# High and low parts of queries and keys: made once on all 128 partitions, put in place by transfers within SBUF

## The chip, the cores and the metric

The kernel runs on one core of one Trainium2 chip. The metric is the device time of one execution in microseconds. Three timed runs of the kernel before took 2474.62, 2475.18 and 2477.01 us; the median, 2475.18 us, is what the change is measured against.

## The reference

One layer of a streaming encoder, in float32: 2048 tokens, width 1024, 16 heads of 64. With `DEPTH = 1` only the chunked attention runs, followed by a SwiGLU network, each between two RMS norms.

```python
def chunk_relpos_attention(h, w_qkv, w_o, rel_bias):     # chunks of 64; each sees itself and the 8 before
    q, k, v = split_heads(h, w_qkv)
    for c in range(n_chunks):
        k0, k1 = max(0, (c - LEFT_CHUNKS) * CHUNK), (c + 1) * CHUNK
        sc = einsum('bhqd,bhkd->bhqk', q[c], k[:, :, k0:k1]) / 8 + bias
        outs.append(einsum('bhqk,bhkd->bhqd', softmax(sc), v[:, :, k0:k1]))
    return merge_heads(outs) @ w_o

def reference(x, ...):
    x = x + rms_norm(chunk_relpos_attention(rms_norm(x, g0), ...), g1)
    return x + rms_norm((silu(h @ w_gate) * (h @ w_up)) @ w_down, g3)     # h = rms_norm(x, g2)
```

## The kernel before

Every float32 product is made from rounded parts. A number is split into a high part (ACT copies it into the type float32r) and a low part (what is left, a subtraction on DVE), and a product is the three matmuls of L188 to L190: high by high, high by low, low by high.

The tokens are taken in two groups (g) of 1024, each of two halves (s) of 512. A group goes through the dense layers and the attention, eight pairs (p) of heads one after the other. For each pair and half `qk_job` makes the queries, then the keys: 24 matmuls of 128x512 into one PSUM bank (tile `mm`, two buffers in the attention stages), with head 0 of the pair on partitions 0 to 63 and head 1 on 64 to 127. ACT copies the bank to a tile `t` in SBUF (L467), and `keep_qk` makes from `t` the operands of the scores:

- `q`, 128 x 4 x 512: on partitions 0 to 63 the high part of the head's queries, on 64 to 127 the high part again; beside it the low part, on both halves too. Per head: two ACT copies (L479, L482), one DVE subtraction (L480) and one POOL copy (L481), all on 64 partitions.
- `k`, 128 x 2 x 1536: per head the high part on partitions 0 to 63 (L493, ACT) and the low part on 64 to 127 (L494, DVE). The first 512 columns are the last half of the group before, loaded from `kh`.

So one matmul over 128 partitions sums high queries by high keys and high queries by low keys (L531), and a second one does the same with the low queries (L532). `Attend.scores` does that for a block of 128 queries; the scores of a block go into one tile `st` (one buffer). DVE adds the bias and takes the row's maximum (L540), ACT makes exponentials (L544), POOL scales them by the reciprocal sum (L548). `transposed` turns the probabilities on TensorE into `tt` (L564, L575; two buffers), DVE and ACT copy them to `pT` (L567, L569, L576), and `output` multiplies by the values (L593).

TensorE's order is written out by hand: a loop over slots, four per job (a job is one half of one pair), puts the scores of the next block, pieces of dense work (`fill`), transposes and outputs one behind the other. The dense work for a job, `qk` above all, has a due slot, shortly before the job's first scores; `until(("qk", ...))` makes sure that it stands ahead of them. On the other engines a scheduler orders the instructions when the program is built, SP's transfers too; each engine works its own list in order. On SP, and so on one hardware queue, stand all loads and stores: weights (`raw`, each half waits for its buffer until the half before has been split, L124 and L125), bias tiles, `kh`, attention results (`attn`, `al`), sums. The shared buffers `io` (three) hold `t` and many loads; `q` and `k` have two buffers each.

After attention comes the network (from about 1110 us on), which the change does not touch.

Of the kernel before, what the change touches and what calls it, by code (L numbers as in the profile page):

```python
# [9 lines left out]
F32 = mybir.dt.float32  # L10
F32R = mybir.dt.float32r
AF = mybir.ActivationFunctionType
ALU = mybir.AluOpType
# [3 lines left out]
P = 128  # L17
# [6 lines left out]
HALF = 512  # L24
# [23 lines left out]
def trunk(  # L48
# [12 lines left out]
    pe, act, dve, pool = nc.tensor, nc.scalar, nc.vector, nc.gpsimd  # L61
# [12 lines left out]
    xp = ctx.enter_context(tc.tile_pool(name="xp", bufs=2))  # L74
# [103 lines left out]
    def dense_bank(n, wide=False):  # L178

        if "psf" in phase and n % 2:  # L180
            return phase["psf"].tile([P, HALF], F32, tag="pd", name="mm", bufs=6)
        if wide and n % 2:
            return phase["psa"].tile([P, 4, P], F32, tag="tt", name="mm", bufs=2).rearrange("p a b -> p (a b)")
        return ps.tile([P, HALF], F32, tag="mm", name="mm")

    def products(pt, a_hi, a_lo, b_hi, b_lo, first, last, go_on=False):

        pe.matmul(pt, a_hi, b_hi, start=first, stop=False, skip_group_check=go_on)  # L188
        pe.matmul(pt, a_hi, b_lo, start=False, stop=False, skip_group_check=go_on)  # L189
        pe.matmul(pt, a_lo, b_hi, start=False, stop=last, skip_group_check=go_on)  # L190
# [24 lines left out]
    def scratch(name):  # L215

        n = turn[0] % 9
        if "fp" in phase:
            turn[0] += 1
        if "fp" in phase and n >= 4:  # L220
            return phase["fp"].tile([P, HALF], F32, tag="tmp", name=name, bufs=5)
        return xp.tile([P, 640], F32, tag="sc", name=name, bufs=4)
# [120 lines left out]
    def hb_tile(n, dtype=F32R, shape=(2, 4, HALF)):  # L343

        n_ht[0] += 1
        pool_ = hp if n < 4 else phase["fp"]
        return pool_.tile([P, *shape], dtype, tag=f"hb{n}", name=f"hb{n}_{n_ht[0]}", bufs=1)
# [63 lines left out]
    heads = (slice(0, 64), slice(64, 128))  # L411
# [7 lines left out]
    def bias_tile(n, h):  # L419

        if len(bias_bufs) < 4:
            t = phase["ap"].tile([P, 640], F32, name=f"bias{h}", bufs=1)
            pool.memset(t[0:64, 0:64], -BIG)
            pool.memset(t[64:128, 576:640], -BIG)
            bias_bufs.append(t)
        t = bias_bufs[n % 4]
        for n, c in enumerate((slice(64, 640), slice(0, 576))):
            e = ext_d[h : h + 1, 64 * n + c.start : 64 * n + c.start + 1]
            sp.dma_start(
                t[64 * n : 64 * n + 64, c],  # L430
                bass.AP(tensor=e.tensor, offset=e.offset, ap=[[1, 64], [1, c.stop - c.start]]),
            )
        return t
# [22 lines left out]
    def qk_job(g, s, p, w):  # L456
        ht = hts[s]
        for which in range(2):
            pt = dense_bank(which, (s, p) == (0, 0))
            c = slice(which * P, which * P + P)  # L460
            for k in range(KT):
                products(
                    pt, w.hi(k, c), w.lo(k, c), ht.hi(k), ht.lo(k), k == 0, k == KT - 1
                )
                yield 3 * C512
            t = xp.tile([P, HALF], F32, tag="io", name="t", bufs=3)
            act.activation(t, pt, AF.Copy, scale=(0.125, 1.0)[which])  # L467
            keep_qk(g, s, p, which, t)

    def keep_qk(g, s, p, which, t):  # L470

        ap = phase["ap"]
        a, b = heads
        if which == 0:

            q = ap.tile([P, 4, HALF], F32R, tag="q", name=f"q_{g}_{s}_{p}", bufs=2)
            qs[g, s, p] = q
            for h, own in enumerate(heads):
                act.activation(q[a, h, :], t[own, :], AF.Copy)  # L479
                dve.tensor_tensor(q[a, 2 + h, :], t[own, :], q[a, h, :].bitcast(F32), op=ALU.subtract)  # L480
                pool.tensor_scalar(q[b, h, :], t[own, :], 1.0, 1.0, op0=ALU.mult, op1=ALU.mult)  # L481
                act.activation(q[b, 2 + h, :], q[a, 2 + h, :].bitcast(F32), AF.Copy)  # L482
            return

        here = slice((s + 1) * HALF, (s + 2) * HALF)
        if s == 0:
            kk = ap.tile([P, 2, 3 * HALF], F32R, tag="k", name=f"k_{g}_{p}", bufs=2)
            ks[g, p] = kk
            if g > 0:
                sp.dma_start(kk[:, :, 0:HALF].bitcast(F32), khist_d[g - 1][p])  # L490
        kk = ks[g, p]
        for h, own in enumerate(heads):
            act.activation(kk[a, h, here], t[own, :], AF.Copy)  # L493
            dve.tensor_tensor(kk[b, h, here], t[own, :], kk[a, h, here].bitcast(F32), op=ALU.subtract)  # L494
        if s == 1 and g + 1 < NG:
            sp.dma_start(khist_d[g][p], kk[:, :, here].bitcast(F32))

    class Attend:
# [14 lines left out]
        def scores(self, ib):  # L513
            g, s, p = self.g, self.s, self.p
            ap = phase["ap"]
            if (g, p, "bias") not in bias:
                bias[g, p, "bias"] = [bias_tile(NH * g + 2 * p + h, 2 * p + h) for h in range(2)]
            q, kk = qs[g, s, p], ks[g, p]
            cols = slice(ib * P, ib * P + P)
            if self.prev:  # L520
                n, k0 = 640, s * HALF + ib * P
                cuts = [(P, 512, 768), (768, 1024, 1408)]
            else:
                n, k0 = (ib + 1) * P, HALF
                cuts = [(0, n), (512, 512 + n)]
            st = phase["psa"].tile([P, 3 * HALF], F32, tag="S", name="st", bufs=1)
            for h in range(2):
                c0 = cuts[h][0]
                for a, b in zip(cuts[h][:-1], cuts[h][1:]):
                    key = slice(k0 + a - c0, k0 + b - c0)  # L530
                    pe.matmul(st[:, a:b], q[:, h, cols], kk[:, h, key], start=True, stop=False)  # L531
                    pe.matmul(st[:, a:b], q[:, 2 + h, cols], kk[:, h, key], start=False, stop=True)  # L532
            for h in range(2):
                c0 = cuts[h][0]
                sc = scratch("sc")
                nmax = ap.tile([P, 1], F32, tag="nmax", name="nmax", bufs=4)
                rows = ap.tile([P, 2], F32, tag="rows", name="rows", bufs=4)
                t = bias[g, p, "bias"][h]
                rev = t[:, n - 1 :: -1] if n == 640 else t[:, 0:n][:, ::-1]
                dve.tensor_tensor_reduce(  # L540
                    out=sc[:, :n], in0=st[:, c0 : c0 + n], in1=rev, scale=-1.0, scalar=3.0e38,
                    op0=ALU.add, op1=ALU.min, accum_out=nmax,
                )
                act.activation(  # L544
                    sc[:, :n], sc[:, :n], AF.Exp, bias=nmax, scale=-1.0, accum_out=rows[:, 0:1]
                )
                dve.reciprocal(rows[:, 1:2], rows[:, 0:1])  # L547
                last_pool[0] = pool.tensor_scalar(  # L548
                    sc[:, :n], sc[:, :n], rows[:, 1:2], 1.0, op0=ALU.mult, op1=ALU.mult
                )  # L550
                self.sc[ib, h] = sc
# [576 lines left out]
    def begin(weights):  # L1128

        ap = phase["ap"]  # L1130
        a, b = heads
        u = Cols(0)
        stage = hb_tile(2, F32, (KT, HALF))
# [6 lines left out]
        for k in range(KT):  # L1140
            if k % 2 == 0:
                s = slice(k * 256, k * 256 + 512)
                sp.dma_start(raw[:, s], plan[0][:, s])
                to = ready[0][k // 4]
                part = slice(k % 4 * 256, k % 4 * 256 + 512)
                split_part(to[0][:, part], to[1][:, part], raw[:, s])
            h = stage[:, k, :]
# [8 lines left out]
        for c in range(2):  # L1156
            s = slice(c * 1024, c * 1024 + 1024)
            part = raw[:, 2048 + c * 1024 : 3072 + c * 1024]
# [9 lines left out]
        for which in range(2):  # L1168
            pt = ps.tile([P, HALF], F32, tag="mm", name="pqk")
# [16 lines left out]
        for t2 in range(2):  # L1186
            pt = phase["psa"].tile([P, 2, 256], F32, tag="tt", name="pv_", bufs=2)
# [9 lines left out]
        ts = []  # L1197
        for which in range(2):
            t = xp.tile([P, HALF], F32, tag="io", name="t", bufs=3)
# [1 line left out]
            ts.append(t)  # L1201
        drain()
        for which in range(2):
            keep_qk(0, 0, 0, which, ts[which])
        weights.extend((qw, vw))
        again = Prep(0, x[0], PRE_MIX)
        again.r = rstd
# [2 lines left out]
    def dense():  # L1210

        halves = [slice(0, HALF), slice(HALF, GROUP)]
        for g in range(NG):
            for p in range(NPAIR):
# [29 lines left out]
                for s in range(2):  # L1244
                    yield from qk_job(g, s, p, qw)
                    said.add(("qk", g, s, p))
# [245 lines left out]
```

## Time and profile before

| | |
|---|---|
| median of three runs | 2475.18 us |
| the profiled execution's own time | 2472.72 us |
| its span, first to last instruction | 2470.8 us |
| PE busy | 2412.7 us, 98% |
| DVE, ACT, POOL busy | 1515.2, 1149.3, 352.2 us |
| moved by DMA | 440.14 MB |
| mean granted TensorE clock | 0.993 |

The page lists, for groups of instructions, line, engine, operation, output and input, shape, count, then the busy time and the mean of one, then how long the engine stood idle just before them and what ended that. "PEld" is the load of weights into TensorE, which overlaps its matmuls; "SPq" is SP issuing a transfer. A busy time of PE counts pipelined matmuls, whose records overlap; where PE truly waited, a timeline row has the wait and its releaser in brackets at its end.

### The profile page before, as it was taken

How to read it: one execution, taken by the hardware profiler on the slowest of the kernel's cores; microseconds unless marked ns; L12 is line 12 of the kernel's file. 1: busy time of each engine (PE TensorE's matmuls, PEld its weight loads, DVE VectorE, ACT ScalarE, POOL GpSimd, SP SyncE). 2: the span in 40 equal slices, each digit the busy share in tenths (PEclk: the TensorE clock that was granted, in tenths of full speed). 3: DMA queues.
4: the chain of work that ended last, by engine and by line, in shares of the span. 5: the costliest groups of instructions: out<-in, count | busy, mean ns of one | idle time of the engine just before them, and what ended most of it. 6: DMA issues, size and time to landing. Idle time of an engine off the chain costs nothing.

```text
span 2470.8 us, 34560 instructions
## 1 busy us (share of the span) xinstructions
PE 2412.7 (98%) x12536; PEld 1996.1 (81%) x12536; DVE 1515.2 (61%) x2616; ACT 1149.3 (47%) x1991; POOL 352.2 (14%) x434
## 2 busy tenths in 40 slices
PE   7999999899999999999999999999999999999997
PEld 5888878688878887878888888888888888888886
DVE  6655455567565655568566655577656655555567
ACT  5545454554555545464433343356443333334444
POOL 3223233301333332220000000000000000000001
PEclk9999999999999999999999999999999999999999
DMA  5336666855666654347667755377667665457654
GB/s 176 120 111 164 147 167 165 247 182 166 156 165 168 155 137 118 82 121 242 187 206 223 251 172 187 99 251 246 206 221 249 203 204 158 132 175 235 195 188 149
DMA packets 184794, 440.14 MB, mean 178 GB/s; under 512 B 20752, under 2 KB 22816, under 8 KB 183344
## 3 DMA queue, kind: packets, MB, share of 16 engines
q1 hardware_dynamic: 174832, 403.33, 50.4%
q0 software_dynamic: 9792, 34.61, 8.6%
q8 instruction: 99, 1.62, 0.3%
q14 instruction: 71, 0.58, 0.1%
HBM read 358.64 MB, written 148.42 MB: 205 GB/s over the span
## 4 chain that ended last, share of the span: by engine, by line
PE 52%; DVE 1%; DMA 1%; issue 0%; ACT 0%; DVEq 0%; SPq 0%; ACTq 0%
PE pd L189 5%; PE pd L188 5%; PE pd L190 5%; PE pb L188 5%; PE pb L189 5%; PE pb L190 5%; PE pa L188 3%; PE pa L190 3%; PE pa L189 3%; PE pc L188 3%; PE pc L190 3%; PE pc L189 3%; PE mm L188 1%; PE mm L190 1%; PE mm L189 1%; DMA raw<-gu_S 0%
## 5 line engine op out<-in xcount | busy, mean ns | idle before, releaser
L188 PE MATMUL mm<-hb,whi 128*128 128x512 f32 x720 | 298.5, 415 | 2.4 <-ACT hb L340 2.4
L189 PE MATMUL mm<-hb,whi 128*128 128x512 f32 x720 | 284.2, 395 | 2.6 <-DVE hb L341 1.8
L190 PE MATMUL mm<-hb,wlo 128*128 128x512 f32 x720 | 284.2, 395 | 0.0
L548 POOL TENSOR_SCALAR sc<-sc,rows 128x640 f32<-128x640 f32 (+4 forms) x256 | 194.7, 765 | 602.4 <-DVE rows L547 548.6
L544 ACT ACTIVATE sc<-sc,nmax 128x640 f32<-128x640 f32 (+4 forms) x256 | 193.2, 755 | 187.1 <-DVE nmax L540 185.5
L540 DVE CUSTOM_DVE_ANT_0 sc<-st,bias 128x640 f32<-128x640 f32 (+4 forms) x256 | 180.3, 738 | 99.7 <-PE st L532 97.3
L188 PE MATMUL pb<-hb,whi_gu_T 128*128 128x512 f32 x528 | 206.3, 391 | 3.1 <-DVE terms L952 3.1
L190 PE MATMUL pb<-hb,wlo_gu_T 128*128 128x512 f32 x528 | 205.5, 389 | 0.0
L189 PE MATMUL pb<-hb,whi_gu_T 128*128 128x512 f32 x528 | 205.5, 389 | 0.0
L258 POOL TENSOR_TENSOR rs<-ms,neg_half 128x4 f32<-128x4 f32 (+1 forms) x12 | 16.9, 1410 | 1233.8 <-DVE ms L256 1233.7
L188 PEld LDWEIGHTS mm<-hb,whi 128*128 128x128 f32 x720 | 136.3, 189 | 37.7 <-issue 14.6
L190 PEld LDWEIGHTS mm<-hb,wlo 128*128 128x128 f32 x720 | 136.1, 189 | 29.8
L189 PEld LDWEIGHTS mm<-hb,whi 128*128 128x128 f32 x720 | 136.7, 190 | 25.4 <-DVE hb L341 3.2
L188 PE MATMUL mm<-whi,hb 128*128 128x256 f32 x480 | 143.2, 298 | 0.0
L189 PE MATMUL pd<-a,whi_d_T 128*128 128x512 f32 (+1 forms) x368 | 140.0, 380 | 0.6 <-DVE a L341 0.6
L188 PE MATMUL pd<-a,whi_d_T 128*128 128x512 f32 (+1 forms) x368 | 140.1, 381 | 0.4 <-ACT a L340 0.4
L190 PE MATMUL pd<-a,wlo_d_T 128*128 128x512 f32 (+1 forms) x368 | 139.8, 380 | 0.0
L188 PE MATMUL pa<-hb,whi_gu_B 128*128 128x512 f32 x352 | 137.5, 391 | 1.4 <-ACT terms L933 1.4
L531 PE MATMUL st<-k,q 128*128 128x384 f32 (+1 forms) x448 | 133.0, 317 | 5.1 <-DVE nmax L540 2.1
L190 PE MATMUL pa<-hb,wlo_gu_B 128*128 128x512 f32 x352 | 137.0, 389 | 0.0
L189 PE MATMUL pa<-hb,whi_gu_B 128*128 128x512 f32 x352 | 137.0, 389 | 0.0
L189 PE MATMUL mm<-wlo,hb 128*128 128x256 f32 x480 | 136.3, 284 | 0.0
(225 smaller groups left out, 5800.2 us busy)
## 6 DMA issues: line engine op xcount, KB each, us to landing
raw<-gu_S SPq DMA_DIRECT2D x88, 512.0 KB, 3.8
raw<-in_w_gu SPq DMA_DIRECT2D x66, 512.0 KB, 4.2
y<-y SPq DMA_DIRECT2D x96, 256.0 KB, 3.8
gu_S<-in_w_gu SPq DMA_DIRECT2D x44, 512.0 KB, 5.4
raw_a<-aT SPq DMA_DIRECT2D x88, 256.0 KB, 3.7
raw_d<-d_S SPq DMA_DIRECT2D x88, 256.0 KB, 3.6
raw<-in_w_a SPq DMA_DIRECT2D x40, 512.0 KB, 4.4
aT<-T SPq DMA_DIRECT2D x66, 256.0 KB, 4.2
```

What stands on the lines that cost most here:

```text
L188: pe.matmul(pt, a_hi, b_hi, start=first, stop=False, skip_group_check=go_on)
L189: pe.matmul(pt, a_hi, b_lo, start=False, stop=False, skip_group_check=go_on)
L190: pe.matmul(pt, a_lo, b_hi, start=False, stop=last, skip_group_check=go_on)
L258: pool.tensor_tensor(r[0][:, :nb], m[:, :nb], neg_half.to_broadcast([P, nb]), op=ALU.pow)
L531: pe.matmul(st[:, a:b], q[:, h, cols], kk[:, h, key], start=True, stop=False)
L540: dve.tensor_tensor_reduce(out=sc[:, :n], in0=st[:, c0 : c0 + n], in1=rev, scale=-1.0, scalar=3.0e38, op0=ALU.add, op1=ALU.min, accum_out= ...
L544: act.activation(sc[:, :n], sc[:, :n], AF.Exp, bias=nmax, scale=-1.0, accum_out=rows[:, 0:1])
L548: last_pool[0] = pool.tensor_scalar(sc[:, :n], sc[:, :n], rows[:, 1:2], 1.0, op0=ALU.mult, op1=ALU.mult)
```

## The change

`keep_qk` gets the PSUM bank itself instead of a copy in SBUF. It makes the high part once, for both heads on 128 partitions, with an ACT copy from PSUM (which also scales), and the low part once with a DVE scalar-tensor-tensor that reads the same bank. Both go into a new tile `stage`, 128 x 2 x 512, with two buffers. Four transfers on SP then copy it into the operand: for `q` each head's high and low rows to both halves of the partitions (64 rows of 4 KB each), for `k` each part of each head to its half (64 rows of 2 KB). The columns of `q` are ordered high, low, high, low, and the two score matmuls read them so. For the first half of the first pair, whose result is scaled by the norm first (`t`, L1200 of before), `keep_qk` gets that tile.

```diff
-            t = xp.tile([P, HALF], F32, tag="io", name="t", bufs=3)
-            act.activation(t, pt, AF.Copy, scale=(0.125, 1.0)[which])
-            keep_qk(g, s, p, which, t)
+            keep_qk(g, s, p, which, pt)
 
-    def keep_qk(g, s, p, which, t):
+    def keep_qk(g, s, p, which, t, scale=None):
         ap = phase["ap"]
         a, b = heads
+        scale = (0.125, 1.0)[which] if scale is None else scale
+        stage = ap.tile([P, 2, HALF], F32R, tag="stage", name=f"stage_{g}_{s}_{p}_{which}", bufs=2)
+        act.activation(stage[:, 0, :], t, AF.Copy, scale=scale)
+        dve.scalar_tensor_tensor(
+            stage[:, 1, :], t, scale, stage[:, 0, :].bitcast(F32), op0=ALU.mult, op1=ALU.subtract
+        )
+        stage = stage.bitcast(F32)
         if which == 0:
             q = ap.tile([P, 4, HALF], F32R, tag="q", name=f"q_{g}_{s}_{p}", bufs=2)
             qs[g, s, p] = q
             for h, own in enumerate(heads):
-                act.activation(q[a, h, :], t[own, :], AF.Copy)
-                dve.tensor_tensor(q[a, 2 + h, :], t[own, :], q[a, h, :].bitcast(F32), op=ALU.subtract)
-                pool.tensor_scalar(q[b, h, :], t[own, :], 1.0, 1.0, op0=ALU.mult, op1=ALU.mult)
-                act.activation(q[b, 2 + h, :], q[a, 2 + h, :].bitcast(F32), AF.Copy)
+                for half in heads:
+                    sp.dma_start(q[half, 2 * h : 2 * h + 2, :].bitcast(F32), stage[own])
             return
...
         for h, own in enumerate(heads):
-            act.activation(kk[a, h, here], t[own, :], AF.Copy)
-            dve.tensor_tensor(kk[b, h, here], t[own, :], kk[a, h, here].bitcast(F32), op=ALU.subtract)
+            for part, half in enumerate(heads):
+                sp.dma_start(kk[half, h, here].bitcast(F32), stage[own, part, :])
...
-                    pe.matmul(st[:, a:b], q[:, h, cols], kk[:, h, key], start=True, stop=False)
-                    pe.matmul(st[:, a:b], q[:, 2 + h, cols], kk[:, h, key], start=False, stop=True)
+                    pe.matmul(st[:, a:b], q[:, 2 * h, cols], kk[:, h, key], start=True, stop=False)
+                    pe.matmul(st[:, a:b], q[:, 2 * h + 1, cols], kk[:, h, key], start=False, stop=True)
...
-            keep_qk(0, 0, 0, which, ts[which])
+            keep_qk(0, 0, 0, which, ts[which], 1.0)
```

TensorE's list is the same row for row. The other lists move. First DVE around the keys of pair 3 in group 1, first half (`k_1_3`), before (`t` is the SBUF copy, `sc` and `nmax` the scores with their bias and maximum, `pT` the transposed probabilities):

```order
L540 ISA sc_7828,nmax_7829<-st_7812,bias1_751 128x640
L540 ISA nmax_7829 128x1
L547 RECIPROCAL rows_7823<-rows_7823 128x1
L567 COPY pT_7710<-tt_7843 128x4x128
L547 RECIPROCAL rows_7830<-rows_7830 128x1
L494 TENSOR_TENSOR k_1_3_7857<-t_7855,k_1_3_7857 64x512 x2
L576 COPY pT_7710<-tt_7878 128x2x128
```

and the same place of DVE's list in the change:

```order
L543 ISA sc_7785,nmax_7786<-st_7769,bias1_751 128x640
L543 ISA nmax_7786 128x1
L550 RECIPROCAL rows_7780<-rows_7780 128x1
L570 COPY pT_7670<-tt_7800 128x4x128
L550 RECIPROCAL rows_7787<-rows_7787 128x1
L475 SCALAR_TENSOR_TENSOR stage_1_0_3_1_7812<-mm_7730,stage_1_0_3_1_7812 128x512
L579 COPY pT_7670<-tt_7836 128x2x128
```

One subtraction of 128x512 from PSUM stands where two of 64x512 from SBUF stood, between the same neighbours. Now SP's list at the same pair, before (`kh` is the key history of the next pair, `sum` and `d_S` are loads and weight sums for the network):

```order
L68 DMA k_1_4_8251<-kh_4_0_123 128x2x512
L68 DMA d_S4_154<-in_w_d 128x1024
L68 DMA sum_7873<-x1_1_84 128x512
L68 DMA bias0_746<-ext_d_155 64x576 x2
L68 DMA bias1_751<-ext_d_155 64x576 x2
L68 DMA d_S3_153<-in_w_d 128x1024
L68 DMA sum_7986<-x1_1_84 128x512
```

and in the change:

```order
L68 DMA q_1_0_3_7725<-stage_1_0_3_0_7722 64x1024 x4
L68 DMA k_1_4_8205<-kh_4_0_123 128x2x512
L68 DMA bias0_746<-ext_d_155 64x576 x2
L68 DMA bias1_751<-ext_d_155 64x576
L68 DMA k_1_3_7815<-stage_1_0_3_1_7812 64x512 x4
L68 DMA bias1_751<-ext_d_155 64x576
L68 DMA d_S3_153<-in_w_d 128x1024
L68 DMA q_1_1_3_7899<-stage_1_1_3_0_7896 64x1024 x4
```

The four transfers of the keys now stand in SP's list behind the next pair's key history and three of its four bias loads.

## The prediction

> **What bounds the kernel now.** I read the page's first section, then the windows by stage.
>
> ```profile
> span 2470.8 us, 34560 instructions
> PE 2412.7 (98%) x12536; PEld 1996.1 (81%) x12536; DVE 1515.2 (61%) x2616; ACT 1149.3 (47%) x1991; POOL 352.2 (14%) x434
> ...
> 60.00:1110.00 1050.00, 1025.08 (x6326) 852.75 (x6326) 618.27 (x1367) 566.03 (x1108) 305.16 (x390) 0.99 0.56 151
> ```
>
> The columns of a window are its length, the busy time of PE, PEld, DVE, ACT and POOL, the granted clock, the DMA engines' share and GB/s. TensorE sets the time. In the attention stages (60 to 1110 us), the only place the change touches beyond the start, PE is idle for 1050.0 - 1025.1 = 24.9 us. ACT and DVE are busy there for 54% and 59%, so work saved on them is worth at most a part of those 24.9 us, and what a half-speed clock adds to them. What PE waits for there, from the waits of that stretch (us in total, times, longest):
>
> ```profile
> PE tt L575 <- ACT pT L569: 7.7, 5, 2.1
> PE tt L575 <- DVE pT L567: 3.1, 4, 2.0
> ...
> PE st L531 <- DVE k L494: 0.9, 2, 0.6
> ```
>
> Two facts matter. Transposes wait for late copies of probabilities on ACT and DVE, 10.8 us. And the scores (L531) wait for the new keys hardly at all, 0.9 us. So the question is whether keys that now come by a transfer still arrive in time.
>
> **What goes.** The groups of instructions that are removed, and the PSUM copy that takes the place of one of the two new ones (count, then busy us and mean ns):
>
> ```profile
> L480 DVE TENSOR_TENSOR q<-t,q 64x512 fp32r<-64x512 f32 x64 | 54.0, 843 | 16.0 <-ACT q L479 14.9
> L481 POOL TENSOR_SCALAR q<-t 64x512 fp32r<-64x512 f32 x64 | 52.5, 821 | 71.1 <-ACT t L467 40.8 <-PE st L532 23.1 <-DVE t L1200 4.0
> L494 DVE TENSOR_TENSOR k<-t,k 64x512 fp32r<-64x512 f32 x64 | 44.9, 702 | 13.4 <-ACT k L493 11.8
> L479 ACT ACTIVATE q<-t 64x512 fp32r<-64x512 f32 x64 | 40.3, 630 | 19.3 <-PE st L532 17.9
> L493 ACT ACTIVATE k<-t 64x512 fp32r<-64x512 f32 x64 | 40.2, 628 | 1.4
> L482 ACT ACTIVATE q<-q 64x512 fp32r<-64x512 f32 x64 | 38.6, 627 | 10.7 <-DVE q L480 9.3
> L467 ACT ACTIVATE t<-mm 128x512 f32<-128x512 f32 x62 | 36.4, 588 | 27.2 <-PE mm L190 26.9
> ...
> 34.88 1.29 DVE L1200 SCALAR_TENSOR_TENSOR t<-pqk,rstd 128x512 f32<-128x512 f32 x2 [3.99 <-ACT rstd L271]
> ```
>
> ACT loses 40.3 + 40.2 + 38.6 = 119 us; L467 stays, as the writer of the high part. POOL loses 52.5. DVE loses 54.0 + 44.9 = 98.9 and gains 64 subtractions that read PSUM. The nearest is L1200, a scalar-tensor-tensor with a PSUM operand of this size, 1.29 us for two, so 0.65 each and 41 us: a net loss of 57. All of it lies beside PE. The PSUM bank is now held until DVE is through, 0.65 us longer. The other bank's 24 matmuls cover that: they start 0.23 us apart (rows 787.50 and 787.72 below), 5.5 us in all. Without that cover it would be 64 times 0.65, 42 us, and I count nothing.
>
> **What comes.** 64 tiles with four transfers each, 256 issues on SP: 32 x 4 x 256 KB for q and 32 x 4 x 128 KB for k, 50 MB. By the page's third section 403.33 MB fill 50.4% of the span, so 50 MB fill 6.3% of 2470.8, 155 us, all inside the 1050: the share there goes from 0.56 to about 0.71. The trace has no transfer within SBUF, so its time is bounded by these rows (KB, median us from issue to landing; then SP's own time for one issue):
>
> ```profile
> aB<-b SPq DMA_DIRECT2D x22, 256.0 KB, 2.1
> attn<-ot SPq DMA_DIRECT2D x28, 256.0 KB, 3.1
> bias<-ext_d SPq DMA_DIRECT2D x64, 144.0 KB, 4.8
> gt<-in_gains SPq DMA_DIRECT2D x1, 16.0 KB, 1.7
> ...
> 453.06 0.32 SPq L68 DMA_DIRECT2D attn<-ot  x1
> ```
>
> Low end 1.7 (16 KB, the shortest of all), high end 4.8 (144 KB, issued at the joins of two pairs, among other loads). I take 3.1: `attn<-ot` leaves SBUF, in this stage, on this queue. In this stage it takes 1.0 us more than `aB<-b`, a store of the same size in the FFN.
> The Trainium skill, "DMA: Bandwidth & Descriptors", section "Anatomy of one DMA", gives about 2.0 us fixed and bytes over 436e3, fitted on the other descriptor path; that would be 2.3 us for 128 KB (an estimate), and 4 us less in the stalls below. The `attn<-ot` row lies above it.
>
> **The path that this lengthens.** Four copies of k in the second group and one in the first come just before the scores that read them. Here the pair p=3 of group 1: ACT's and DVE's rows, then PE's (start us, length us):
>
> ```profile
> 787.15 0.58 ACT L467 ACTIVATE t<-mm 128x512 f32<-128x512 f32 x1
> 788.44 1.40 DVE L494 TENSOR_TENSOR k<-t,k 64x512 fp32r<-64x512 f32 x2 [1.47 <-ACT k L493]
> 787.50 0.39 PE L188 MATMUL mm<-hb,whi 128*128 128x512 f32 x1
> 787.72 0.39 PE L189 MATMUL mm<-hb,whi 128*128 128x512 f32 x1
> 789.46 0.28 PE L531 MATMUL st<-k,q 128*128 128x256 f32 x1
> ```
>
> The first score that needs new keys (the second piece of head 0, 256 wide) starts 789.46 - 787.15 = 2.31 us after the copy out of PSUM began. The old way was ready by then: copy, high part, subtraction. The new way needs 0.58 (ACT) + 0.65 (DVE) + about 0.2 between engines = 1.4 us, and then 3.1 us from the issue of the low part: 4.5. Head 1's low part is issued two issues, 0.65 us, later, of which 0.47 is covered by head 0's scores: 0.2 more. Stall: 4.5 - 2.3 + 0.2 = 2.4 us. The other four joins:
>
> ```profile
> 434.54 0.58 ACT L467 ACTIVATE t<-mm 128x512 f32<-128x512 f32 x1
> 436.55 0.33 PE L531 MATMUL st<-k,q 128*128 128x128 f32 x1 [0.59 <-DVE k L494]
> 659.98 0.57 ACT L467 ACTIVATE t<-mm 128x512 f32<-128x512 f32 x1
> 663.46 0.28 PE L531 MATMUL st<-k,q 128*128 128x256 f32 x1
> 916.25 0.58 ACT L467 ACTIVATE t<-mm 128x512 f32<-128x512 f32 x1
> 918.58 0.28 PE L531 MATMUL st<-k,q 128*128 128x256 f32 x1
> 1042.64 0.57 ACT L467 ACTIVATE t<-mm 128x512 f32<-128x512 f32 x1
> 1046.13 0.28 PE L531 MATMUL st<-k,q 128*128 128x256 f32 x1
> ```
>
> At 434.54 PE would be there after 1.4 us (436.55 less its wait of 0.59): 4.5 - 1.4 + 0.4 less the 0.9 already waited, 2.6. At 659.98 3.5 us pass: 1.0 + 0.2 = 1.2. At 916.25 2.3 pass: 2.4. At 1042.64 3.5: 1.2. Sum of the five: 2.4 + 2.6 + 1.2 + 2.4 + 1.2 = 9.8 us. With a landing of 1.7 it is 1.0 + 1.2 + 0 + 1.0 + 0 = 3.2; with 4.8 it is 9.8 + 5 x 1.7 = 18.3. PE's order is unchanged, so nothing fills the gap. What stands behind the waiting score on PE is the dense work of the next group: the loss is whole.
>
> A stall can cost more than its length (windows as above, the last but two columns the clock):
>
> ```profile
> 264.50:267.90 3.40, 3.40 (x16) 3.40 (x15) 1.37 (x4) 0.00 (x0) 0.00 (x0) 0.50 0.84 290
> 689.00:692.40 3.40, 3.40 (x20) 2.97 (x19) 1.91 (x6) 0.72 (x1) 1.58 (x3) 1.00 0.83 227
> ```
>
> A wait of 1.95 us (before 264.26, its row is below) is followed by 3.4 us at a clock of 0.50, which costs 1.7 us. Just before 689, too, PE waited about 2 us for a transpose's buffer, and the clock stayed at 1.00. Between these two I give a stall over 2 us two chances in three: 3 x 2/3 x 1.7 = 3.4 us.
> The Trainium skill, "TensorE: Matmul & The Clock Gate", Part 1, says the array falls to half speed after an idle window of about 3.4 us that runs free; by that rule no stall here would throttle and the 3.4 us would go. The trace disagrees, 0.50 after a wait of 2 us, and I follow the trace.
>
> **What the relief is worth.** The case at 264:
>
> ```profile
> 260.87 1.06 ACT L124 ACTIVATE whi<-raw 128x1024 fp32r<-128x1024 f32 x1 [2.39 <-DMA raw<-in_w_a]
> ...
> 262.45 1.28 ACT L493 ACTIVATE k<-t 64x512 fp32r<-64x512 f32 x2
> 263.64 0.57 ACT L569 ACTIVATE pT<-tt 128x512 f32<-128x512 f32 x1
> 264.26 0.48 PE L575 MATMUL tt<-ident,sc 128*128 128x128 f32 x2 [1.95 <-ACT pT L569]
> ```
>
> ACT waits for a weight load, and the copy of probabilities (L569) stands behind L493. Without L493 PE's wait falls from 1.95 to 0.7, and the half-speed stretch goes: 1.3 + 1.7 = 3.0 us. The other waits of this kind begin with the weight load too, and most have no q or k work between; I add 2: relief 5 us. Against that, weight loads share the DMA engines with 27% more traffic (0.71 over 0.56):
>
> ```profile
> ACT whi L124 <- DMA raw<-in_w_a: 28.1, 15, 5.3
> ...
> SPq L68 <- DVE wlo L125: 249.4, 45, 23.0
> ```
>
> 28.1 / 15 = 1.9 us each, a quarter more is 0.5, and four of them reach PE: 2 us. The second row is SP's own: it is an in-order queue that stands still up to 23 us behind a weight load that waits for its buffer. At the five joins the rows ahead of the new transfers are bias, key-history and activation loads that had been issued by then, so I add nothing, but this is where more could come from.
>
> **Sum.** 9.8 + 3.4 + 2 - 5 = +10 us. The profiled execution took 2472.72 (span 2470.8 and 1.9 around it), so 2483; the runs' median is 2475.18, 2.5 above it, so 2485.5. I say 2486.
>
> **Rivals.**
> Congested transfers. At a join SP has just sent the next pair's bias and key-history loads (the order of its rows shows them), and landings of 4.8 are measured for exactly those bias loads. Then the stalls are 18.3, the throttling 5 x 2/3 x 1.7 = 5.7, the weight loads 4, less 5: +23, 2498. For it: the 4.8. Against: the store `attn<-ot` in the same stage takes 3.1. If SP is blocked at one join by a weight load, 5 to 8 us more.
> Cover. Landing near 2.1, as `aB<-b` has, makes the stalls 1.4 + 1.6 + 0.2 + 1.4 + 0.2 = 4.8, with hardly a throttle, and relief of 5 cancels it: 2475 to 2477. Against: the 3.1.
> Faster. The in-order queues of ACT and DVE run ahead after each late weight load, and the 10.8 us that L575 waits fall to 3, with two half-speed stretches (1.7 each) gone: 11 us. It decides if the landing is under 2.0, where the stalls are 3 to 4: 2475 - 7 = 2468. For it: L493 in the rows at 264. Against: it needs both the shortest landing and that most L575 waits have q or k work in front of them.
>
> **Chances.** The forecast (stalls of 1 to 3 us at the five joins, 2481 to 2493) 0.48; congested 0.17; cover 0.20; faster 0.15. A measurement here can tell 0.2%, 5 us, from nothing: slower by more 0.64, within 0.21, faster 0.15. The range is 2468 to 2506: from the faster case to the congested one with SP blocked once.
>
> **What would show it.** Right: in the waits of 60 to 1110, L531 waiting for DMA k in a handful of places, up to 3 us and 8 to 12 in total; ACT about 119, POOL 52 and DVE 55 us less busy; a new row of 64x512 transfers landing in about 3 us; clock 0.5 stretches after two or three of the joins; the DMA share of 60 to 1110 near 0.71. Wrong: L531 waits for DMA under 5 us, or landings under 2, or a loss elsewhere, for instance SP waiting on a stage tile, ACT waiting for a stage buffer, or PE waiting for a PSUM bank.

## The result and the profile after

The changed kernel takes 2504.31 us (median of four runs, 2499.38 to 2508.8), beside 2474.9 us of the kernel before in the same comparison: a ratio of 1.0125, 95% interval 1.0094 to 1.0156. It is slower, as forecast, but by 29 us and not by 10. The profiled execution took 2505.02 us.

The page's first rows of the changed kernel, and then the attention stages from the windows (length, busy time of PE, PEld, DVE, ACT and POOL, granted clock, DMA share, GB/s). The last score matmul of the attention starts at 1099.3 us before and at 1129.1 in the change, so the window ends at 1140 where it ended at 1110:

```profile
span 2503.2 us, 34787 instructions
...
PE 2417.7 (97%) x12536; PEld 2001.3 (80%) x12536; DVE 1462.9 (58%) x2552; ACT 1034.8 (41%) x1801; POOL 295.0 (12%) x370
```

```profile
60.00:1140.00 1080.00, 1033.49 (x6334) 859.84 (x6334) 567.98 (x1307) 458.61 (x926) 251.73 (x330) 0.98 0.72 193
```

ACT is 115 us less busy than before, POOL 57, DVE 52: the work is gone as said. Nearly all of the loss lies in the attention: its last score comes 29.7 us later, in a span that is 32.4 longer. PE's idle time there was 24.9 us and is now 1080.0 - 1033.5 = 46.5, which is 21.6 more, and PE is busy 8.4 us longer, over nearly the same number of recorded matmuls. Who PE waits for, from the waits of 60 to 1140 (us in total, times, longest):

```profile
PE st L534 <- DMA k<-stage: 28.5, 11, 6.0
PE tt L578 <- DVE pT L570: 9.2, 8, 2.6
PE tt L578 <- ACT pT L572: 2.9, 1, 2.9
```

The scores wait for the transfers of the keys: 28.5 us, where the keys made on DVE cost 0.9. Where it happens, from PE's timeline (start, length, in brackets the wait just before it):

```profile
442.97 0.44 PE L534 MATMUL st<-k,q 128*128 128x128 f32 x1 [5.98 <-DMA k<-stage]
444.85 0.45 PE L534 MATMUL st<-k,q 128*128 128x128 f32 x1 [1.21 <-DMA k<-stage]
474.44 0.35 PE L534 MATMUL st<-k,q 128*128 128x256 f32 x1 [2.90 <-DMA k<-stage]
672.78 0.53 PE L534 MATMUL st<-k,q 128*128 128x384 f32 x1 [4.23 <-DMA k<-stage]
803.88 0.55 PE L534 MATMUL st<-k,q 128*128 128x256 f32 x1 [4.91 <-DMA k<-stage]
939.38 0.55 PE L534 MATMUL st<-k,q 128*128 128x256 f32 x1 [4.79 <-DMA k<-stage]
1072.82 0.58 PE L534 MATMUL st<-k,q 128*128 128x256 f32 x1 [3.30 <-DMA k<-stage]
```

These are the five joins of the prediction, and one place more, the second half of the pair at the first of them (474.44). The join of pair 3 in group 1 in the timeline rows of ACT and DVE:

```profile
796.51 0.58 ACT L474 ACTIVATE stage<-mm 128x512 fp32r<-128x512 f32 x1
797.12 0.69 DVE L475 SCALAR_TENSOR_TENSOR stage<-mm,stage 128x512 fp32r<-128x512 f32 x1 [0.80 <-ACT stage L474]
```

and SP's issues around it:

```profile
793.40 0.58 SPq L68 DMA_DIRECT2D k<-kh  x1
794.38 1.76 SPq L68 DMA_DIRECT2D bias<-ext_d  x3
797.11 2.48 SPq L68 DMA_DIRECT2D k<-stage  x4
```

Both parts are made 1.30 us after the copy began (797.12 + 0.69 - 796.51), a little sooner than the 1.4 that I had put down. SP issues the first of the four transfers at once, and without its wait the score would have started at 803.88 - 4.91 = 798.97, 2.46 us after the copy began. So at this join neither the engines' part nor SP is late. The landings, from the list of DMA issues (KB, median us from issue to landing): first of the whole program, then of the window 797 to 800 with the four of this join, then of 602 to 605 with three others:

```profile
q<-stage SPq DMA_DIRECT2D x128, 256.0 KB, 5.4
k<-stage SPq DMA_DIRECT2D x128, 128.0 KB, 5.5
...
k<-stage SPq DMA_DIRECT2D x4, 128.0 KB, 6.1
...
k<-stage SPq DMA_DIRECT2D x3, 128.0 KB, 2.3
```

The same transfer takes 2.3 us in one place and 6.1 in another. What differs, from the windows of those two stretches (last but one number: share of the DMA engines' time):

```profile
602.00:605.00 3.00, 3.00 (x28) 3.00 (x27) 3.00 (x5) 0.60 (x1) 0.00 (x0) 1.00 0.79 182
797.00:803.80 6.80, 1.97 (x11) 1.35 (x9) 1.81 (x3) 0.72 (x2) 1.02 (x2) 0.91 1.06 253
```

By that measure the DMA engines are full in this join. But the share alone does not tell the two cases apart: at the join of pair 7 it is 0.77 (1067.2 to 1072.8 us), and the four transfers there take 5.3 to 6.0 us.

Behind each of the six waits of 2.9 us or more PE runs at half its clock, here after those at 474.44 and 939.38:

```profile
474.90:478.30 3.40, 3.21 (x10) 2.50 (x9) 1.75 (x4) 2.14 (x5) 0.00 (x0) 0.51 0.78 248
939.20:946.00 6.80, 6.10 (x21) 5.18 (x21) 2.23 (x6) 1.73 (x4) 0.80 (x1) 0.50 0.41 109
```

What does tell a short landing from a long one stands in POOL's list. Not all transfers stand on SP: POOL sends part of the weight sums for the network itself, nearly all of 512 KB (`gu_S`, `d_S`), on a queue of its own. At the join of pair 1 such a sum leaves between the second and the third of the keys' transfers. The issues in order of time, then the landing of the first two transfers and of the last two:

```profile
664.64 1.19 SPq L68 DMA_DIRECT2D k<-stage  x2
665.54 0.83 POOL L843 DMA_DIRECT2D gu_S<-in_w_gu  x1
665.87 1.23 SPq L68 DMA_DIRECT2D k<-stage  x2
...
k<-stage SPq DMA_DIRECT2D x2, 128.0 KB, 2.4
...
k<-stage SPq DMA_DIRECT2D x2, 128.0 KB, 5.7
```

At pair 5 the sum leaves 0.05 us after the first of the four, which lands in 2.5 us; the other three take 6.3 in the median. At the other three joins a sum leaves with the first transfer or is still under way when it leaves. These sums leave at the same places in the kernel before, too, 0.7 to 1.5 us after ACT's copies at 659.98, 787.15 and 916.25 that the prediction shows:

```profile
661.48 0.83 POOL L840 DMA_DIRECT2D gu_S<-in_w_gu  x1
787.81 0.85 POOL L840 DMA_DIRECT2D gu_S<-gu_S  x1
916.91 0.84 POOL L840 DMA_DIRECT2D d_S<-in_w_d  x1
```

### The profile page after: what moved, and what is told of

The parts are those of the page before. It is cut to its first block, busy times and chain, and to the rows that moved or that the text cites. A ratio compares the mean times of both kernels' runs of the same rounds, so it can differ in the third digit from the quotient of the medians.

```text
span 2503.2 us, 34787 instructions
## 1 busy us (share of the span) xinstructions
PE 2417.7 (97%) x12536; PEld 2001.3 (80%) x12536; DVE 1462.9 (58%) x2552; ACT 1034.8 (41%) x1801; POOL 295.0 (12%) x370
## 4 chain that ended last, share of the span: by engine, by line
PE 47%; DMA 4%; DVE 2%; issue 1%; ACT 0%; SPq 0%; DVEq 0%; ACTq 0%
PE pd L189 5%; PE pd L188 5%; PE pd L190 5%; PE pb L188 4%; PE pb L190 4%; PE pb L189 4%; PE pa L188 3%; PE pa L189 3%; PE pa L190 3%; PE pc L188 3%; PE pc L189 3%; PE pc L190 3%; DMA res<-in_x 1%; PE mm L188 1%; PE mm L190 1%; PE mm L189 1%
## 5 line engine op out<-in xcount | busy, mean ns | idle before, releaser
L551 POOL TENSOR_SCALAR sc<-sc,rows 128x640 f32<-128x640 f32 (+4 forms) x256 | 189.1, 740 | 736.0 <-DVE rows L550 699.0
L534 PE MATMUL st<-k,q 128*128 128x384 f32 (+1 forms) x448 | 135.8, 322 | 28.5 <-DMA k<-stage 28.5
L125 DVE TENSOR_TENSOR wlo<-raw,whi 128x1024 fp32r<-128x1024 f32 x76 | 94.0, 1236 | 74.5 <-ACT whi L124 74.2
```

The lines of the kernel that those rows point to most:

```text
L125: dve.tensor_tensor(lo, raw, hi.bitcast(F32), op=ALU.subtract)
L534: pe.matmul(st[:, a:b], q[:, 2 * h, cols], kk[:, h, key], start=True, stop=False)
L551: last_pool[0] = pool.tensor_scalar(sc[:, :n], sc[:, :n], rows[:, 1:2], 1.0, op0=ALU.mult, op1=ALU.mult)
```

## The experiments

The first theory is the prediction's: the loss is the late keys at the joins. Its first rival is that the traffic of the queries, twice that of the keys, costs the time. Once the keys were found to be the larger part, three causes of their late landing stood against each other: SP's in-order queue (Q below), DMA engines that are full at that moment (D below), and a transfer of this shape that takes so long whatever else runs (I below).

### Keys by engines, queries by transfers

The keys are made as before: copy to SBUF, then ACT and DVE on 64 partitions.

```diff
+        elif (g, s, p) != (0, 0, 0):
+            pt, t = t, xp.tile([P, HALF], F32, tag="io", name="t", bufs=3)
+            act.activation(t, pt, AF.Copy, scale=scale)
...
-            for part, half in enumerate(heads):
-                sp.dma_start(kk[half, h, here].bitcast(F32), stage[own, part, :])
+            act.activation(kk[a, h, here], t[own, :], AF.Copy)
+            dve.tensor_tensor(kk[b, h, here], t[own, :], kk[a, h, here].bitcast(F32), op=ALU.subtract)
```

> One part undone: the keys are made as before (copy out of PSUM, two high parts on ACT, two subtractions on DVE, straight into their places); only the queries go through the stage tile and the 128 transfers of 256 KB. Theory A (the keys' transfers are late at the joins, and that is nearly all of the loss): the score matmuls no longer wait for a transfer, the five long waits of 3 to 6 us before them are gone, and the time is 2468 to 2478 us, no slower than before. Theory B (the added traffic and SP's longer list slow the weight loads and everything else; 33 of the 50 MB are still there): two thirds of the loss stay, 2490 to 2497 us.

Measured: 2481.74 us, ratio 1.0034 (1.0023 to 1.0046). No wait for a transfer of keys is left. PE's longest waits from 60 to 1120:

```profile
PE tt L582 <- ACT pT L576: 8.3, 3, 5.1
PE pssq L254 <- DVE total L240: 7.5, 1, 7.5
```

and ACT's wait for the weight loads in the same answer:

```profile
ACT whi L124 <- DMA raw<-in_w_a: 38.2, 20, 5.5
```

About 7 us of loss remain with the queries' transfers alone. The rows are of an execution of 2487.02 us, 5 above the median, and show waits of PE in several places. ACT's wait is 38.2 us where it was 28.1, and the transposes wait for ACT as they did. So here the relief of ACT and POOL is worth less than what the rest of the queries' change costs. ACT's longer wait does not show that the weight loads cost it: with less work ACT also gets to them sooner. What the 7 us are owed to is not shown.

### Queries by engines, keys by transfers

```diff
-                for half in heads:
-                    sp.dma_start(q[half, 2 * h : 2 * h + 2, :].bitcast(F32), stage[own])
+                act.activation(q[a, 2 * h, :], t[own, :], AF.Copy)
+                dve.tensor_tensor(q[a, 2 * h + 1, :], t[own, :], q[a, 2 * h, :].bitcast(F32), op=ALU.subtract)
+                pool.tensor_scalar(q[b, 2 * h, :], t[own, :], 1.0, 1.0, op0=ALU.mult, op1=ALU.mult)
+                act.activation(q[b, 2 * h + 1, :], q[a, 2 * h + 1, :].bitcast(F32), AF.Copy)
```

> The other part undone: the queries are made as before on ACT, DVE and POOL; only the keys go through the stage tile and the 128 transfers of 128 KB. Theory A: the late keys are still there, 2488 to 2503 us; if the landing of 5.5 us came from the queries' traffic it falls towards 3 to 4 us and the waits of the scores from 28 to about 15 us; if the landing is what such a transfer takes, it stays above 5 and the waits near 28. Theory B: one third of the traffic stays, 2480 to 2486 us.

Measured: 2497.18 us, ratio 1.0091 (1.0068 to 1.0115). The wait for the keys from 60 to 1140:

```profile
PE st L540 <- DMA k<-stage: 29.1, 11, 6.1
```

and the window of the same stretch (columns as above):

```profile
60.00:1140.00 1080.00, 1038.37 (x6391) 861.00 (x6390) 603.73 (x1349) 536.22 (x1054) 298.92 (x390) 0.99 0.61 166
```

The keys' wait is there in full, at the same joins, though the queries' two thirds of the new traffic are gone and the share of the stage fell from 0.72 to 0.61. What was expected of the landing held only for the median: over the whole program it fell from 5.5 to 3.9 us, but of the transfers at the joins only those of pair 7 became short (2.9, for 5.5 in the change). The two losses against the runs of before beside them, 7.4 and 22.9 us, add up to 30, about what the whole change loses: three quarters belong to the keys.

### The keys' transfers on ACT's queue

```diff
-                sp.dma_start(kk[half, h, here].bitcast(F32), stage[own, part, :])
+                act.dma_start(kk[half, h, here].bitcast(F32), stage[own, part, :])
```

> The change whole, but the keys' four transfers per tile are issued by ACT on its own queue instead of SP's; the queries' stay on SP. What is asked is why a landing at the joins takes 5 to 6 us. Theory Q (the transfers stand in SP's queue behind bias and history loads issued just before them): on a queue of their own they land in 2.5 to 3.5 us, the scores' waits for them fall from 28 to 10 to 14 us, the time to 2485 to 2492 us. Theory D (the sixteen DMA engines themselves are full at the joins, whoever issues): landings stay at 4.5 to 6 us, the waits at 22 to 30 us, the time at 2496 to 2508 us.

Measured: 2506.62 us, ratio 1.0136 (1.0121 to 1.0152). The landing of the keys, from the list of DMA issues:

```profile
k<-stage ACTq DMA_DIRECT2D x128, 128.0 KB, 6.5
```

and the wait for them from 60 to 1140:

```profile
PE st L534 <- DMA k<-stage: 35.1, 13, 8.1
```

One more wait, of 7.1 us at pair 5, the profile puts down to a `d_S` transfer; the keys landed there just 0.1 us before the score began. On a queue with nothing of SP's ahead of them the transfers land later, not sooner. SP's order is not the cause. The Trainium skill, "DMA: Bandwidth & Descriptors", section "Issuing engines are not separate DMA queues", says that transfers run on the same 16 DMA engines whichever engine starts them; these rows are in line with it.

### Without most of the bias loads

```diff
+        if n >= 4:
+            return t
```

> The change whole, but the bias tiles are loaded for the first four heads only and kept: 60 of the 64 tiles' loads of 144 KB are left out, and the other heads get a wrong bias. Those loads stand ahead of the keys' transfers at the joins. If they are what fills the DMA engines there (Theories Q and D with the bias as the traffic), the waits of the scores for the keys fall from 28 to 10 to 16 us and the time to 2484 to 2493 us. If a transfer within SBUF from 64 partitions takes 5 us by itself (Theory I), the waits stay at 25 to 30 us and the time above 2497 us.

Measured: 2503.55 us, ratio 1.0121 (1.0104 to 1.0138). The wait for the keys from 60 to 1140:

```profile
PE st L536 <- DMA k<-stage: 28.7, 9, 7.9
```

The bias loads, three of whose four SP sends just ahead of the keys at a join, are not what makes these late. This speaks against the way in which my "congested" rival had argued.

### The sums of weights sent in the first group's time

About a third of the bytes moved from 590 to 1110 us belong to sums of FFN weights (`gu_S`, `d_S`, nearly all of 512 KB), which are spread over both groups of tokens. The edit asks for all of them in the first group's time, in the change whole and in the kernel with engine-made queries. In the traces it does so in part: of 66 issues between 590 and 1110 us, 23 are left in the first kernel and 21 in the second, the last at 767 and 756 us. So the join of pair 1 still has sums beside it, and those of pairs 3, 5 and 7 have none.

```diff
-                if m > 4 and (m * n_sums) // 120 > ((m - 1) * n_sums) // 120:
+                if m > 4 and (m * n_sums) // 58 > ((m - 1) * n_sums) // 58:
```

> The change whole, but all sums of FFN weights (512 KB copies and accumulating transfers, some 65 issues between 590 and 1110 us) are sent in the first group's time, so the second group runs without them; the four joins of the second group keep every instruction of the change. In the changed kernel the keys' wait in 590 to 1110 is 18.2 us in 7 places, the share there 0.71 and the landing 5.7. Theory D (a landing is long because the DMA engines are full at that moment): share in 590 to 1110 falls to 0.4 to 0.5, the landing to 2.3 to 4, the keys' wait there to 9 or less. Theory I (a transfer between halves of SBUF of this shape takes 5 to 6 us whatever else runs at a join): wait there stays at 16 to 20. The total can go either way, since the first group gets twice the traffic (its share was 0.78 already): 2485 to 2515 by D, 2500 to 2525 by I; the window decides, not the total.

> As the kernel whose queries are written by engines and whose keys alone go by transfers (2497.18; keys' wait in 590 to 1110 18.0 us in 8 places, share 0.58, landing 4.1), with all sums of FFN weights sent in the first group's time. Theory D: share in 590 to 1110 falls to 0.25 to 0.4, landing to 2.2 to 3, the keys' wait there to 3 to 8 (with a landing of 2.3 the five stalls of the prediction's working sum to about 5, four of them here). Theory I: 15 to 20 stays. Total 2480 to 2500 by D, 2495 to 2515 by I.

Measured: 2500.81 us, ratio 1.0102 (1.008 to 1.0124), and 2492.56 us, ratio 1.0069 (1.0048 to 1.009). Of the first kernel, in 590 to 1110, the wait for the keys:

```profile
PE st L534 <- DMA k<-stage: 12.5, 7, 3.2
```

their landing, from the list of DMA issues:

```profile
k<-stage SPq DMA_DIRECT2D x64, 128.0 KB, 3.7
```

In the second group the wait falls from 18.2 to 12.5 us, the landing from 5.7 to 3.7 and the share from 0.71 to 0.53. Over the whole attention less is gained: in this execution (2506.79 us, the longest of four) the keys' wait is 23.7 for 28.5, with one of 7.1 us at the first group's join, and the transposes wait 17.9 for 13.1. In the second kernel the wait is 12.8 us for 18.0 and the landing 2.9 for 4.1. The landings are as D expected, the share of the first kernel and both waits are above what D expected, and the waits lie below what Theory I expected.

What is left of the sums explains why. From 760 us on hardly one is left. There, of the second kernel, PE's wait for the keys and their landing over 40 transfers:

```profile
PE st L540 <- DMA k<-stage: 6.4, 6, 2.6
...
k<-stage SPq DMA_DIRECT2D x40, 128.0 KB, 2.4
```

The kernel with engine-made queries and the sums in both groups has 12.8 us and 3.1 in that stretch. In the first kernel the wait there is 7.0 us and the landing 3.3, where the changed kernel has 13.8 and 5.4. Before 760 us, where the sums are left, the wait is no shorter (6.4 for 5.2 in the second kernel, 5.6 for 4.4 in the first).

The joins one by one say the same. In the second kernel, the landing of the four transfers at the joins of pairs 5 and 7, from the DMA issues of a window around each (930 to 942, 1055 to 1066), and PE's waits there, from the timeline:

```profile
k<-stage SPq DMA_DIRECT2D x4, 128.0 KB, 3.1
...
k<-stage SPq DMA_DIRECT2D x4, 128.0 KB, 2.3
...
938.42 0.36 PE L540 MATMUL st<-k,q 128*128 128x256 f32 x1 [2.09 <-DMA k<-stage]
...
1062.32 0.36 PE L540 MATMUL st<-k,q 128*128 128x256 f32 x1 [0.50 <-DMA k<-stage]
```

At pair 3 the landing is 3.6 and the wait 2.62. At pair 1 a sum of POOL leaves at 673.42, again between the second and the third transfer: the first two land in 3.5 us, the last two in 6.5, and the score waits 4.17 us, about as long as in the change (4.23). So Theory I falls: nothing in the shape of the transfer needs 5 us. And the load that makes most of the difference is found: the weight sums in flight at the same moment. Whether it is their size or the queue that POOL sends them on was not tested apart. Other loads count too: without any sum the landing at pairs 3 and 5 is still 3.8 and 4.1 us in the first kernel.

### The due slot of the dense work moved earlier

The same table of due slots, with queries and keys due 2.5 slots ahead of their job where it was 1.4, in the change whole, and in the kernel before as a control. From the start of ACT's copy to the first score that reads the keys, the score's own wait left out, the traces have 7.9 to 11.1 us at the five joins where the change has 1.4 to 3.7.

```diff
-                due.append((4 * i - 1.4 if kind == "qk" else 4 * i + 4, total))
+                due.append((4 * i - 2.5 if kind == "qk" else 4 * i + 4, total))
```

> The change whole, all transfers and traffic kept; only the due slot of the queries and keys in TensorE's written order is moved from 1.4 to 2.5 slots ahead, which puts 9 to 11 us of other matmuls between a key group's end and its scores at the five joins (3.0 to 3.7 before). Theory A: the scores find their keys there, waits for the keys' transfers fall from 28 to under 5 us and the time to 2465 to 2476 us. Theory B: the traffic is unchanged, so the time stays at 2490 to 2504 us.

> Control: the kernel before with the same earlier due slot and nothing else. If the earlier slot is worth little by itself, 2468 to 2478 us, within 0.3% of the kernel before; if it falls by 10 us or more, the gain of the earlier slot in the changed kernel is not owed to the keys' transfers alone.

Measured: the change 2472.65 us, ratio 0.9994 (0.9978 to 1.001); the control 2476.51, ratio 1.0007 (0.9996 to 1.0019). In the first, the window of 60 to 1120:

```profile
60.00:1120.00 1060.00, 1031.77 (x6390) 856.24 (x6389) 573.99 (x1319) 459.14 (x934) 250.55 (x330) 1.00 0.74 200
```

and waits in it, of PE and of ACT:

```profile
PE st L534 <- DMA k<-stage: 2.3, 3, 1.5
PE tt L578 <- DVE pT L570: 12.4, 11, 2.0
...
ACT whi L124 <- DMA raw<-in_w_a: 43.4, 16, 4.8
```

All transfers are kept and the share is as high, but the loss is gone, and the clock of the window is 1.00 again. So the loss lies in the path from the keys to the scores. But the earlier slot does two things at once. At pairs 1, 3 and 5 the transfers now leave between two of POOL's sums, when the earlier one has landed or nearly so, and land in 2.3 to 2.9 us in the median. At the first group's join and at pair 7 some of them still take 6.5 to 7.4, and there the work in front of the score hides them:

```profile
442.07 0.33 PE L534 MATMUL st<-k,q 128*128 128x128 f32 x1 [0.63 <-DMA k<-stage]
...
1042.98 0.38 PE L534 MATMUL st<-k,q 128*128 128x256 f32 x1 [1.46 <-DMA k<-stage]
```

The change had 5.98 and 3.30 us at these two places. The run also shows how little the relief is worth when nothing is lost. With 115 us less on ACT and 57 on POOL the changed kernel takes 3.9 us less than the control with the same order, over ten executions each: at the edge of what these runs can tell from nothing. The transposes still wait 12.4 us for copies of probabilities. ACT's wait for the weight loads is 43.4 us without any loss, so that wait need not cost anything.

### Keys straight from PSUM, without a transfer

The kernel before, with one thing of the change: the keys' parts are made from the PSUM bank. ACT and DVE write them to their places on 64 partitions, as before; only the copy to SBUF goes.

```diff
-            t = xp.tile([P, HALF], F32, tag="io", name="t", bufs=3)
-            act.activation(t, pt, AF.Copy, scale=(0.125, 1.0)[which])
+            t = pt
+            if which == 0:
+                t = xp.tile([P, HALF], F32, tag="io", name="t", bufs=3)
+                act.activation(t, pt, AF.Copy, scale=0.125)
```

> The kernel before with one part of the change alone, the reading of PSUM: the keys' high and low parts are made by ACT and DVE straight from the PSUM bank into their places, without the copy to SBUF and without a transfer; the queries stay as before. It saves 32 ACT copies of 0.59 us (19 us off TensorE's path) and makes the keys ready about 0.6 us sooner. Theory A: 2468 to 2477 us, the same as before or a few us faster; the cost of the change lies in the transfers, not in reading PSUM. If reading PSUM on DVE were the cost (bank held longer), it would be over 2482 us.

> The run above with the due slot moved from 1.4 to 2.5 slots ahead, tried as a version that may beat both kernels: 2464 to 2474 us. By the control run of the earlier slot on the kernel before (2476.5 us) the slot alone brings nothing, so under 2468 us would need the two together.

Measured: 2469.27 us, ratio 0.998 (0.997 to 0.999), the only kernel of the study whose interval lies below the kernel before; with the earlier slot too 2474.05, ratio 1.0005 (0.9993 to 1.0016). A row from the waits of the first, 60 to 1120:

```profile
ACT whi L124 <- DMA raw<-in_w_a: 19.9, 15, 2.8
```

ACT's wait for weight loads is 19.9 us, against 28.1 of before and 43.8 of the change; the row is of the fastest of ten executions, 2463.64 us. The gain is 4 to 5 us and goes away with another order of PE's work, so it is small and depends on that order; why it is there was not tested.

## Why the prediction was right, and where its sizes were off

**What bounds, and the sign.** Right. TensorE sets the time, the loss lies in the attention, and it is the wait of the scores for the keys' transfers. Experiments with the slot (loss gone, all transfers kept) and with the keys on the engines (three quarters gone) show it.

**What goes and what comes.** Right: 115, 57 and 52 us less on ACT, POOL and DVE for 119, 52.5 and 57, the subtraction from PSUM 0.69 us for 0.65, the share 0.72 for 0.71. The held PSUM bank cost PE one wait of 1.2 us where I counted nothing.

**Stalls at the five joins, 9.8 us: the term that was mis-sized.** It measured 28.5, or 27.6 beyond the 0.9 of before, of which 3.1 at a sixth place. The working from a landing to a stall held. In the kernel with engine-made queries and the sums moved, pair 5's landing was 3.1 and the stall 2.09 + 0.23 us, where the prediction had worked out 2.4 for just that landing; at pair 3 a landing of 3.6 gave 2.62 + 0.42 where the same working gives 2.9, and at pair 7 one of 2.3 gave 0.50 + 0.56 where it gives 0.4. The landing was the fault: 3.1 taken, about 5.9 measured for the transfer that each of the five stalls hung on. Five joins at 2.8 more are 14.0 and the sixth place is 3.1, which leaves 0.7 of the 17.8 that were missing. SP's issues took longer than I took them to, too: four in a row take 2.48 us, 0.62 each, not the 0.32 of `attn<-ot`, so head 1's keys leave 1.2 us behind head 0's and not 0.65. I took the landing of another transfer, a median over the whole stage, for one that leaves just when POOL sends a weight sum. The bias row with 4.8 was the nearer one in place, and in the change it is longer itself, 5.9. The prediction looked at SP's list for what stands ahead of the keys and not at POOL's.
The Trainium skill's formula in "DMA: Bandwidth & Descriptors", section "Anatomy of one DMA", gives an estimate of 2.3 us for 128 KB. Without a weight sum in the way the rows at 602 of the change and at pair 7 of the kernel with the sums moved agree with it, 2.3 both. With a sum in flight the same transfer mostly took 5.3 to 6.9 us at the joins of the change; the formula has no term for other traffic.

**Half clock, 3.4 us.** PE is busy 8.4 us more, which I put down to the half clock; no run isolates it. All six places with a wait of 2.9 us or more ran into a stretch at 0.5; I had given a stall over 2 us two chances in three, for three stalls. The mechanism was right, and longer and more stalls made it larger.
The Trainium skill, "TensorE: Matmul & The Clock Gate", Part 1, asks for an idle window of about 3.4 us. The waits of 4.23 to 5.98 us agree with it. The one of 2.90 us at 474.44 does not: 0.51 for the next 3.4 us. Nor does the prediction's wait of 1.95 us.

**Relief, -5 us, and later weight loads, +2.** The relief did not show in these waits. The transposes waited 10.8 us by the two rows of the prediction, which end at 1100 us, and 11.2 up to 1110; in the change it is 12.1. The case at 264 shows how that came about at one place. Without `k` work between, ACT's copy now follows the weight load at once, but ACT waits for that load 4.89 us (up to 265.38) where it waited 2.39, and PE waits 2.86 us for the copy where it waited 1.95. Over the stage ACT's waits for weight loads rose from 28.1 to 43.8 us. Part of that costs nothing, since ACT has less to do and gets there sooner; the landing itself rose from 4.4 to 4.9 us in the median, the half microsecond that the prediction took. SP stood 79.3 us, in 27 places, for the low part of a stage tile, one of the prediction's signs of being wrong; but it did so for 69.4 us with the earlier slot as well, where nothing was lost. PE's idle time for everything but keys did fall, from 24.0 to 18.0 us, but by single waits elsewhere in its list, which I would not call relief.

**The sum.** 27.6 (28.5 less 0.9) + 8.4 - 6.0 = +30.0 us in the attention, where the last score comes 29.7 later. The likeliest time was 2486, in a forecast of 2481 to 2493 that the result missed by 11 us; it lies in the wide range, 2 us below its upper end, and on the rival called congested (2498, or 5 to 8 more), to which I gave 0.17. That the range reached so far is in part luck. The rival's landing of 4.8 was still too short, and its two reasons failed: SP wasn't blocked at a join, which is what the last 5 to 8 us stood for, and without the bias loads the wait was the same. Other traffic did make the transfers late, but it was the weight sums.

**Cover and faster.** Both needed landings near 2 us. Those exist in this kernel, 2.3, at the joins too, but there only for transfers that leave ahead of a weight sum. With the wait gone by other means the time was that of before, which is "cover"; the 3.9 us less than the control are too little to bear out "faster", which stood for 7.

## What to carry to other kernels

A transfer that takes the place of work on a half-idle engine is only free if the consumer has more other work in front of it than the transfer takes at its slowest: here 1.4 to 3.7 us of it cost 28.5 us of waits, and 7.9 to 11.1 cost 2.3. Look up the distance between producer and consumer in the list of the engine that bounds, and move the producer earlier before adding the transfer. Take the landing from transfers sent in the same moment, and look in the lists of all engines that send, not of one, for what else is sent then; do not take it from the row that resembles the transfer in size and direction. And ask first what the relieved engine was holding up: here the relief was worth 4 us at most, and dropping one copy by reading PSUM directly, in one order of PE's work, gave more than the whole change.

## What the runs showed of the hardware

- A transfer of 128 KB within SBUF, 64 rows of 2 KB, landed 2.2 us after its issue at the least and 10.3 at the most in one execution of the change.
- At one join, two of them that left just before a 512 KB transfer of POOL landed in 2.4 us, and two that left just behind it in 5.7.
- The mean share of the DMA engines did not tell a short landing from a long one: 2.3 us at 0.79, and 5.3 to 6.0 us at 0.77.
- Four issues of it in a row take SP 2.48 us, 0.62 each, twice the 0.32 of a 256 KB store of 128 rows.
- Moved to ACT's queue it landed in 6.5 us in the median, against 5.5 on SP's.
- A wait of 2.90 us of PE was followed by 3.4 us at half the clock (0.51).
